# A hybrid decoder block on one core: the segments' openings traced in smaller pieces, B's serial products placed behind A's, and less scratch

## The chip, the core and the metric

The kernel runs on one core of a Trainium2 chip. The metric is the device time of one execution in microseconds (us). Engines are named as in the profile: PE is the matmul engine and PEld its weight loads, DVE the vector engine, ACT the scalar (activation) engine, POOL the GpSimd engine, and SP the engine that here only issues DMAs. Matmuls read from SBUF and write to PSUM, which has eight banks of 512 float32 columns by 128 partitions.

## The reference

One decoder block over 16 meta tokens and 1024 tokens, width 1024, all in float32:

```
h = h + 0.5 * swiglu(rmsnorm(h))                    # FFN 1, hidden width 2816
u = rmsnorm(h)
aq, ak, av, az, beta, alpha, bcols, ga, gb = split(u @ w_in)
o_a = deltanet(aq, ak, av, az, beta, alpha)         # "A": short causal convolution, silu, l2 norm,
                                                    #   chunked gated delta rule, 8 heads of 128
o_b = rwkv7(bcols)                                  # "B": token shift, low-rank decay, a and gate,
                                                    #   state recurrence, 16 heads of 64, group norm
h = h + (sigmoid(ga) * o_a + sigmoid(gb) * o_b) @ w_out
h = h + 0.5 * swiglu(rmsnorm(h))                    # FFN 2
return rmsnorm(h)[meta tokens dropped]
```

A chunk of A: with a triangular inverse T of the chunk, `v_new = u - w @ state`, `o = qg @ state + attn @ v_new`, `state = state * exp(g) + k_tail^T @ v_new`. B's state is carried over chunks of 64 tokens by one product with a chunk matrix.

## The kernel before

Activations lie with channels on partitions and tokens on the free axis. A float32 product is made as three products of rounded halves (high x high, high x low, low x high; `mm3`, recorded at line L262), so one projection of 128 output columns is 24 matmuls of up to 512 tokens; the tile of a projection is called `pp`, its weights `w` (loaded raw by SP as `wraw`, split by ACT L159 and DVE L160), its input tiles `uk`.

The program has three parts: FFN 1 (to about 736 us in the trace), the mixer (`middle`, to about 2300 us) and the output projection with FFN 2. The change touches only the mixer. It goes through two segments of tokens: segment 0 has the 16 meta tokens and 512 tokens (528 columns, done as 272 and 256), segment 1 the other 512. In each segment there are 8 steps, one for each pair of heads of B and one head of A, so 16 steps, numbered through (step 8 is the first of segment 1).

Each step is cut into acts, each a function that traces instructions:

- `new_b`: the low-rank decay (raw weights `upr` loaded, split to `upz`; products `pw` and `pa`; exponentials and a scan `Ls` on ACT and DVE), then B's three projections with the token shift (`vB`, `kB`, `rB`; function `shifted`), a transposition of vB (`vbp`), two column sums of the key (`cs`), and two of the bonus (`bon`).
- `new_a`: A's projections, convolution, silu and l2 norm.
- `operands`: the chunks' small products of both branches (`vap`, `grb`, `gra`, `bkt`, `vp`, `ktp`).
- `inverses`, `merge_blocks`, `transitions`: the triangular inverses, first row by row on DVE (`tb`, `Xb`), then in blocks of 32 and 64 on PE (`iv1` to `iv4`), then the products that make B's chunk matrices (`xp`, `vp`, `mp`, `np`).
- `chains`: the serial part. A has four chunks of 128, each with products p1, p2, pq (twice) and p3: p1, then a subtraction on DVE (`rhA`), p2, a scaling on ACT (`vn`), pq and p3, then the state's update on DVE (`SA`). B has eight chunks of 64, each one product b1 and one DVE operation (`SBs`); `bq` reads all of them.
- `gates` (three projections and `gat`) and `finish` (norms, merge, store).
- `segment(1)` loads and scales the new segment's input, makes `uk`, and calls `lora`, which makes the low-rank inputs shared by the 8 steps (`ws`, `as`, the gate's `gds` and `g3`, and by a scan `c3`, A's log decays) and transposes c3 to tokens on partitions (`tkp`).

The order in which acts are traced is given by the strings FIRST, REGULAR, BEFORE_SWITCH, SWITCH (a plus sign means the next step's). The tile framework's scheduler, at build time, then orders each engine's instructions by the traced order and its own model of durations; on the chip each engine runs its list in that order, and waits on semaphores. Tiles are allocated from pools: a tile's next use waits until its last reader is done. Scratch tiles of 528 columns come from one tag `tmp` with 8 slots. The projections' PSUM tiles come from `main_banks` (L239): two tiles of two banks in segment 0, three tiles of one bank in segment 1; two more banks serve the chains.

## Time and profile before

| what | us |
|---|---|
| median of 3 runs (range) | 3064.41 (3064.28 to 3066.05) |
| the profiled execution, its own time | 3063.9 |
| its span in the trace | 3062.1 |
| PE busy | 2946.3 |
| DVE busy | 2017.1 |
| ACT busy | 1377.8 |
| one step of segment 1, from `iv1` to `iv1` (1924.1 to 2011.1) | 87 |

A row of the order of time gives start, length, engine, line, operation, output and inputs by the program's names, the number of records, and in brackets how long the engine had been idle and what ended that. The rows count most matmuls twice, since a float32 product with plain operands is two passes. A row of a stretch gives its length, the busy time of PE, PEld, DVE, ACT and POOL with the number of records, the clock that was granted to PE (1.00 is full speed), the DMA share and GB/s. The granted clock is 0.99 over the whole execution.

### The profile page before, as it was taken

The numbers are of one execution on the slowest core, as the hardware profiler recorded it, in microseconds if no ns is written. First come the engines' busy times: TensorE is split into PE (matmuls) and PEld (weight loads), VectorE is DVE, ScalarE is ACT, GpSimd is POOL, SyncE is SP. The second block draws the span as 40 slices with busy tenths as digits, with TensorE's granted clock in tenths as the row PEclk, the third lists the DMA queues.
The fourth block names the chain that finished last, engine by engine and source line by source line (L and its number), as shares of the span: only waits on it lengthen the run. The fifth ranks groups of instructions, "written<-read, shape, count | busy, mean of one in ns | idle before, by whom it ended". The sixth has DMA issues, their size and how long they took to land. (4 is left out here: it accounts for less than half of the span.)

```text
span 3062.1 us, 61716 instructions
## 1 busy us (share of the span) xinstructions
PE 2946.3 (96%) x25498; PEld 2531.0 (83%) x25498; DVE 2017.1 (66%) x3872; ACT 1377.8 (45%) x2404; POOL 336.1 (11%) x503
## 2 busy tenths in 40 slices
PE   8999999999899999999999999999999999999998
PEld 8999998998778887888776777777777888888886
DVE  7555554346668877788768888877866765556335
ACT  5322222125555656566566556665644432223114
POOL 0322220000000000000000000000000022222000
PEclk9999999999999999999999999999999999999999
DMA  3232224234232322323323332233354232225223
GB/s 124 84 98 84 84 81 160 80 98 143 69 75 72 83 62 73 79 79 87 89 85 81 78 81 70 79 82 85 104 152 167 71 108 90 83 83 197 61 78 115
DMA packets 257594, 287.20 MB, mean 94 GB/s; under 512 B 169296, under 2 KB 175440, under 8 KB 257312
## 3 DMA queue, kind: packets, MB, share of 16 engines
q1 hardware_dynamic: 253072, 271.43, 30.2%
q0 software_dynamic: 2512, 8.65, 0.8%
q8 instruction: 201, 3.29, 0.5%
q10 hardware_dynamic: 1728, 3.16, 0.3%
q14 instruction: 81, 0.66, 0.1%
HBM read 232.70 MB, written 50.47 MB: 92 GB/s over the span
## 5 line engine op out<-in xcount | busy, mean ns | idle before, releaser
L262 PE MATMUL pp<-uk,w 128*128 128x512 f32 (+2 forms) x4824 | 969.0, 347 | 11.4 <-DVE w L160 7.4
L262 PEld LDWEIGHTS pp<-uk,w 128*128 128x128 f32 x4824 | 748.6, 191 | 105.9 <-DVE w L160 9.4
L159 ACT ACTIVATE w<-wraw 128x1024 fp32r<-128x1024 f32 (+2 forms) x330 | 326.5, 990 | 522.8 <-PE pd L262 296.8
L262 PE MATMUL pd<-hd,w 128*128 128x512 f32 (+2 forms) x2448 | 455.4, 347 | 5.5 <-ACT hd L159 3.7
L160 DVE TENSOR_TENSOR w<-wraw,w 128x1024 fp32r<-128x1024 f32 (+2 forms) x330 | 404.3, 1226 | 67.9 <-ACT w L159 57.2
L262 PEld LDWEIGHTS pd<-hd,w 128*128 128x128 f32 x2448 | 392.7, 190 | 64.0 <-ACT hd L159 3.9
L449 PE MATMUL pg<-bt,w 128*128 128x256 f32 (+2 forms) x2520 | 400.7, 317 | 0.0
L449 PEld LDWEIGHTS pg<-bt,w 128*128 128x128 f32 x2520 | 360.4, 188 | 33.0 <-DVE w L160 0.2
L455 DVE TENSOR_TENSOR c<-c,pg 128x520 f32<-128x520 f32 (+1 forms) x280 | 189.7, 689 | 278.0 <-PE pg L449 250.5
L449 PE MATMUL pg<-b,w 128*128 128x256 f32 (+2 forms) x2160 | 347.8, 317 | 0.0
L449 PEld LDWEIGHTS pg<-b,w 128*128 128x128 f32 x2160 | 309.7, 188 | 28.1
L159 ACT ACTIVATE w<-wrx 128x1024 fp32r<-128x1024 f32 (+1 forms) x64 | 58.5, 913 | 289.8 <-PE pg L449 249.2
L419 POOL TENSOR_TENSOR wrx<-wrx 128x512 f32<-128x512 f32 x38 | 52.5, 1382 | 733.1 <-DVE w22b L160 516.4
L1384 DVE TENSOR_TENSOR tb<-Ub,Xb 115x126 f32<-115x126 f32 (+22 forms) x496 | 124.9, 252 | 9.8 <-DMA Ub<-scr 1.4
L1386 DVE TENSOR_TENSOR Xb<-Xb,tb 115x126 f32<-115x126 f32 (+22 forms) x496 | 125.3, 253 | 8.2
L1193 DVE SCALAR_TENSOR_TENSOR acc<-xr,pk,acc 128x528 f32<-128x528 f32 (+1 forms) x144 | 109.4, 759 | 29.0 <-ACT acc L1189 27.8
L625 DVE SCALAR_TENSOR_TENSOR h<-pd,h 128x528 f32<-128x528 f32 (+1 forms) x64 | 44.6, 698 | 118.0 <-PE pd L262 115.4
L625 DVE SCALAR_TENSOR_TENSOR hh<-pd,hh 128x512 f32<-128x512 f32 x64 | 44.1, 690 | 115.5 <-PE pd L262 114.1
L262 PE MATMUL pwo<-uk,w 128*128 128x512 f32 x384 | 99.1, 408 | 3.4 <-DVE w L160 1.9
L262 PEld LDWEIGHTS pwo<-uk,w 128*128 128x128 f32 x384 | 72.1, 193 | 20.6 <-DVE w L160 2.3
L943 ACT ACTIVATE sh<-pp,pk 128x528 f32<-128x528 f32 (+1 forms) x54 | 37.5, 695 | 99.2 <-PE pp L262 99.1
L160 DVE TENSOR_TENSOR w<-wrx,w 128x1024 fp32r<-128x1024 f32 (+1 forms) x64 | 66.6, 1041 | 14.5 <-ACT w L159 14.3
(400 smaller groups left out, 4184.0 us busy)
## 6 DMA issues: line engine op xcount, KB each, us to landing
wraw<-in_win SPq DMA_DIRECT2D x150, 512.0 KB
wraw<-in_wgu SPq DMA_DIRECT2D x44, 512.0 KB
wrx<-in_wgu SPq DMA_DIRECT2D x44, 512.0 KB
wraw<-in_wdn SPq DMA_DIRECT2D x48, 320.0 KB
wraw<-in_wdn SPq DMA_DIRECT2D x32, 384.0 KB
hid<-c SPq DMA_DIRECT2D x44, 260.0 KB
hr<-hid SPq DMA_DIRECT2D x22, 520.0 KB
hid<-c SPq DMA_DIRECT2D x44, 256.0 KB
```

What stands on the lines that cost most here:

```text
L159: g.nc.scalar.activation(hi, src, AF.Copy)
L160: (eng or g.nc.vector).tensor_tensor(lo, src, hi.bitcast(F32), op=ALU.subtract)
L262: g.nc.tensor.matmul(ps, lhsT=l, rhs=r, start=i == 0, stop=i == n - 1)
L419: sums.tensor_tensor(a22, a21, a22, op=ALU.add)
L449: nc.tensor.matmul(ps[:, c0 : c0 + cn], lhsT=l[:, x, k, :], rhs=r[:, k, y, c0 : c0 + cn], start=i == 0, stop=i == 3 * HK - 1)
L455: nc.vector.tensor_tensor(o, x, y, op=ALU.add)
L625: nc.vector.scalar_tensor_tensor(hv, pd, 0.5, hv, op0=ALU.mult, op1=ALU.add)
L943: nc.scalar.activation(sh[:, 1 : 1 + n], ps, AF.Identity, scale=g.V("mu", i))
L1193: nc.vector.scalar_tensor_tensor(acc[:, :n], xr[:, tap : tap + n], V("convw", ct * 4 + tap), acc[:, :n], op0=ALU.mult, op1=ALU.add)
L1384: nc.vector.tensor_tensor(tv, U[:, i, i + 1 :].unsqueeze(2).to_broadcast([npt, nt, ncc]), X[:, i, 0:ncc].unsqueeze(1).to_broadcast([npt, n ...
L1386: nc.vector.tensor_tensor(X[:, i + 1 :, 0:ncc], X[:, i + 1 :, 0:ncc], tv, op=ALU.add)
```

## The change

Three edits, none of which adds or removes an instruction on any engine.

1. *Openings.* `new_b` is cut in two: `decay` (raw weights, `pw`, `pa`, exponentials, scan and what follows from it) and `new_b` (the rest). From `lora` the transposition of c3 is cut out as `tokens`. The acts are traced in a new order: at the first opening the decay of step 1 comes ahead of the operands of step 0, and `tokens` behind B's projections; at the second opening the PSUM banks are switched ahead of the last gates of segment 0, not behind them, and `tokens` again comes behind `new_b`.
2. *Chain.* B's products b1 are traced to come right behind A's p1 and p2 of each chunk, two to a chunk.
3. *Scratch.* `shifted` writes its result into the shift tile itself, the gate of the convolution goes into the convolution's input tile, and the raw low-rank weights get their own tile of 256 columns with one buffer, shared by the decay and the gates.

```diff
+FIRST = "decay new_b tokens new_a decay+ operands inverses new_b+ new_a+"
-FIRST = "new_b new_a operands inverses", "new_b new_a"
-REGULAR = "merge_blocks transitions operands+ inverses+ chains gates finish new_b++ new_a++"
-BEFORE_SWITCH = "merge_blocks transitions operands+ inverses+ chains gates finish gates+ segment new_b++ new_a++"
+REGULAR = "merge_blocks transitions operands+ inverses+ chains gates finish decay++ new_b++ new_a++"
+BEFORE_SWITCH = "merge_blocks transitions operands+ inverses+ chains gates finish banks gates+ segment decay++ new_b++ tokens++ new_a++"
...
+            elif act == "banks":
+                main_banks(g, 1, S1)
+            elif act == "decay":
+                steps[it] = decay(g, it)
...
-    main_banks(g, *((1, S1) if s else (2, 2)))
+    if s == 0:
+        main_banks(g, 2, 2)
...
-    o = g.st.tile([P, 531], F32, name=name, tag=tag, bufs=NTMP if tag == "tmp" else 1)
-    sh = tmp_tile(g, "sh", 529)
+    sh = tmp_tile(g, name if tag == "tmp" else "sh", 529)
+    o = sh if tag == "tmp" else g.st.tile([P, 531], F32, name=name, tag=tag)
...
-    raw = tmp("upr", 512).rearrange("p (a m) -> p a m", m=P)
-    nc.sync.dma_start(raw[:, 0:2, :], g.a["upwa"][j])
+    raw = st.tile([P, 2, P], F32, name="upr", tag="upr")
+    nc.sync.dma_start(raw, g.a["upwa"][j])
...
-        sg = tmp("sg")
+        sg = xr
...
+        m = nc.tensor.matmul(p1[:, :P], lhsT=kqg[:, 0, csl], rhs=S, start=True, stop=True)
         rh = st.tile([P, P], F32, name="rhA", tag="rhA", bufs=1)
         nc.vector.tensor_tensor(rh, Va[:, i, :], p1[:, :P], op=ALU.subtract)
+        with g.tc.issue_after(m.ins):
+            chunk_b(2 * i)
         p2 = pt("p2")
+        m = nc.tensor.matmul(p2[:, :P], lhsT=Y[:, NCB + i, :], rhs=rh, start=True, stop=True)
+        with g.tc.issue_after(m.ins):
+            chunk_b(2 * i + 1)
...
-    for i in range(NCB):
+    def chunk_b(i):
         ps = pt("b1")
         nc.tensor.matmul(ps[:, :CB], lhsT=g.mt[:, i], rhs=SBs[:, i], start=True, stop=True)
...
-        if i % 2 == 0:
-            chunk_a(i // 2)
+    for i in range(NCA):
+        chunk_a(i)
...
-    raw = tmp_tile(g, "ugr", 512).rearrange("p (a m) -> p a m", m=P)
+    raw = st.tile([P, 2, P], F32, name="ugr", tag="upr")
```

What this makes of the engines' lists. A row is line, operation, output and inputs, shape, and how many in a row; `pp` is a projection. The first place is PE's list at the opening of segment 0, from A's value product of step 0 (`vap`) on. Before:

```order
L1205 MATMUL vap<-ck,acc 128x128 x4
L1210 MATMUL vmp<-ck,acc 16x128
L262 MATMUL pp<-uk,w 128x256 x2
L1231 MATMUL grb<-AR,BK 64x128 x32
L1241 MATMUL gbm<-arm,bkpm 64x16 x2
L1270 MATMUL gra<-kq 128x256 x4
```

and further down, behind the products `bkt`, `vp`, `btp`, `ktp` and `vmp` with no `pp` among them:

```order
L1332 MATMUL vmp<-ck,kq 16x128
L1103 MATMUL pw<-ws,upz 128x256
L1104 MATMUL pw<-ws,upz 128x256
L1107 MATMUL pa<-as,upz 128x256
L1108 MATMUL pa<-as,upz 128x256
L1103 MATMUL pw<-ws,upz 128x272
L1104 MATMUL pw<-ws,upz 128x272
L1107 MATMUL pa<-as,upz 128x272
L1108 MATMUL pa<-as,upz 128x272
L1076 MATMUL vbp<-ck,vB 64x64 x16
```

Now, from the second half of the decay's products on (the first half stands right behind `vap`, too):

```order
L1115 MATMUL pa<-as,upz 128x272
L1116 MATMUL pa<-as,upz 128x272
L261 MATMUL pp<-uk,w 128x256 x2
L1247 MATMUL grb<-AR,BK 64x128 x16
L261 MATMUL pp<-uk,w 128x256 x5
L1247 MATMUL grb<-AR,BK 64x128 x16
L1257 MATMUL gbm<-arm,bkpm 64x16 x2
L1286 MATMUL gra<-kq 128x256 x4
L261 MATMUL pp<-uk,w 128x272 x9
L1296 MATMUL gm<-c3m,ck 16x16
L261 MATMUL pp<-uk,w 128x272 x8
```

The decay's products of step 1 have moved ahead of all of step 0's operands, and 51 projection products stand between `vap` and `vbp`, where there were two.

The second place is PE's list at the opening of segment 1, from the last gates of segment 0 (`gat` closes them) to the decay of step 8. Before:

```order
L262 MATMUL pp<-uk,w 128x512 x24
L1601 MATMUL gat<-gds,ug 128x512 x3
L1601 MATMUL gat<-g_7380,ug 128x512
L262 MATMUL pp<-uk,w 128x512 x103
L999 MATMUL tkp<-ck,c_17710 128x16 x4
L1103 MATMUL pw<-ws,upz 128x512
```

Now:

```order
L261 MATMUL pp<-uk,w 128x512 x29
L1623 MATMUL gat<-gds,ug 128x512 x2
L261 MATMUL pp<-uk,w 128x512 x22
L1623 MATMUL gat<-gds,ug 128x512
L1623 MATMUL gat<-g_7377,ug 128x512
L261 MATMUL pp<-uk,w 128x512 x72
L1111 MATMUL pw<-ws,upz 128x512
```

`tkp` no longer stands ahead of `pw` (it is now behind the first `bon` of step 8), and `gat` stands among the last gate projection. A few projections have changed sides of `gat`; their sum is the same.

The third place is PE's list in a chunk of the chain in a regular step of segment 1. Before:

```order
L1562 MATMUL b_22825<-SBs,mt 128x64
L1542 MATMUL p_22828<-SA,kq 128x128
L262 MATMUL pp<-uk,w 128x512 x3
L1546 MATMUL p_22832<-rhA,Y_7140 128x128
L1550 MATMUL pq<-kq,SA 128x128
L262 MATMUL pp<-uk,w 128x512 x2
L1551 MATMUL pq<-attn,vn 128x128
L1553 MATMUL p_22839<-vn,ktl 128x128
L262 MATMUL pp<-uk,w 128x512
L1562 MATMUL b_22843<-SBs,mt 128x64
```

Now (p1, b1, p2, b1, pq, pq, p3):

```order
L1558 MATMUL p_22720<-SA,kq 128x128
L1583 MATMUL b_22724<-SBs,mt 128x64
L261 MATMUL pp<-uk,w 128x512 x2
L1564 MATMUL p_22727<-rhA,Y_7140 128x128
L1583 MATMUL b_22729<-SBs,mt 128x64
L261 MATMUL pp<-uk,w 128x512 x2
L1570 MATMUL pq<-kq,SA 128x128
L1571 MATMUL pq<-attn,vn 128x128
L1573 MATMUL p_22737<-vn,ktl 128x128
L261 MATMUL pp<-uk,w 128x512 x3
```

B's two products have moved from between p3 and the next p1 into the two links behind p1 and p2, and the cover of each link changed from 3, 2 and 4 or 5 `pp` to 2, 2 and 3. Around step 9, where segment 1's second step begins, 33 `pp` stand between step 8's `bq` and step 9's first `bon`, where there were 59.

More of the change, by code (lines that the diff above doesn't have):

```diff
@@ L170, in schedule @@
     yield "segment", 0
-    for it in range(2):
-        for act in FIRST[it].split():
-            yield act, it
+    for act in FIRST.split():
+        yield act.rstrip("+"), act.count("+")
     for it in range(last + 1):
@@ L1078, in run, with decay @@
     return out
-def new_b(g, it):
+def decay(g, it):
     nc, st, V = g.nc, g.st, g.V
@@ L1125, in new_b @@
         nc.scalar.activation(elm[:, 1:17], Ls[:, 0:16], AF.Exp, scale=-CDEC)
+    q.EN, q.ELx, q.av = EN, ELx, av
+    return q
+def new_b(g, q):
+    nc, st, V, c, j, n, off, it = g.nc, g.st, g.V, q.c, q.j, q.n, q.off, q.it
+    meta = q.s == 0
+    fs = slice(off, off + FULL)
+    tmp = lambda name, w=528: tmp_tile(g, name, w)
+    EN, ELx, av, elm = q.EN, q.ELx, q.av, meta and q.elm
     v = shifted(g, c, 48 + j, 16 + j, "vB")
@@ L1168, in new_b @@
     nc.vector.tensor_tensor(bv, ps, v[:, fs], op=ALU.mult)
-    return q
 def new_a(g, q):
```

16 lines of the change are left out of this document (8 added, 8 removed).

## The prediction

> **What bounds the kernel now.** I read the page's sums first, then the chain that ended last, then the span cut into stretches, and last the order of time on the matmul engine (PE) where a stretch showed idle time.
>
> ```profile
> span 3062.1 us, 61716 instructions
> PE 2946.3 (96%) x25498; PEld 2531.0 (83%) x25498; DVE 2017.1 (66%) x3872; ACT 1377.8 (45%) x2404; POOL 336.1 (11%) x503
> ...
> PE 37%; DVE 3%; ACT 2%; issue 1%; DMA 1%; SPq 0%; DVEq 0%; ACTq 0%
> ```
>
> PE is busy 96% of the span, and the chain is mostly PE. No instruction is added or removed by this change, so it can only win back time in which PE stands still or runs at a lower clock. Where that time lies, by stretches (columns: length, then busy time of PE, weight loads, DVE, ACT, POOL; then the granted clock):
>
> ```profile
> 700.00:900.00 200.00, 178.97 (x1705) 160.67 (x1707) 136.40 (x269) 117.55 (x212) 12.31 (x53) 0.97 0.32 95
> 900.00:1500.00 600.00, 579.42 (x7072) 497.44 (x7063) 465.08 (x1156) 348.43 (x715) 35.82 (x133) 1.00 0.29 77
> 1500.00:1700.00 200.00, 179.95 (x1881) 141.79 (x1880) 146.14 (x322) 122.22 (x220) 17.27 (x37) 0.94 0.30 79
> 1700.00:2300.00 600.00, 579.12 (x6358) 460.22 (x6358) 475.72 (x1132) 348.26 (x669) 34.86 (x90) 1.00 0.35 92
> ...
> 832.07:842.30 10.23, 8.32 (x62) 7.48 (x63) 9.26 (x33) 3.32 (x8) 0.48 (x5) 0.50 0.00 1
> 862.79:866.19 3.40, 3.40 (x17) 3.40 (x16) 3.40 (x12) 1.68 (x4) 0.23 (x2) 0.50 0.78 252
> 1511.32:1514.72 3.40, 3.40 (x9) 2.63 (x9) 3.40 (x10) 2.29 (x4) 0.00 (x0) 0.50 0.42 162
> 1545.46:1552.26 6.80, 4.79 (x15) 4.18 (x16) 2.73 (x6) 2.66 (x5) 0.48 (x2) 0.50 0.04 14
> 1654.68:1664.90 10.22, 6.93 (x16) 5.07 (x16) 10.04 (x24) 5.51 (x10) 0.66 (x1) 0.50 0.28 103
> 1685.40:1688.80 3.40, 3.40 (x67) 3.26 (x68) 2.41 (x8) 0.66 (x2) 0.30 (x1) 0.50 0.17 24
> ```
>
> The two segment openings (700 to 900, 1500 to 1700) have 21.0 and 20.1 us of idle PE in 200 us each; the 1200 us of regular steps between and behind them have 41.5 us, about 3 us in each of some 13 steps. The last six rows are the only stretches of the mixer at half clock, and all lie in the openings. PE's busy time in them is 30.2 us, of which half, 15.1 us, is lost. So the openings hold 41 + 15 = 56 us, and those are the places that the traced order is changed in.
>
> **The first opening.** PE's rows in order of time (start, length, engine, operation, and in brackets the idle time ahead with what ended it):
>
> ```profile
> 736.93 22.85 PE L262 MATMUL pp<-uk,w 128*128 128x272 f32 x183
> 761.25 1.04 PE L999 MATMUL tkp<-ck,c 128*128 128x16 f32 x8 [1.47 <-ACT g L993]
> ...
> 810.19 0.50 PE L262 MATMUL pp<-uk,w 128*128 128x256 f32 x2
> 813.55 1.69 PE L1231 MATMUL grb<-AR,BK 64*64 64x128 f32 x32 [1.70 <-DVE LT L1234]
> 833.25 1.13 PE L1076 MATMUL vbp<-ck,vB 64*64 64x64 f32 x32 [4.70 <-DVE vB L944]
> 836.09 0.61 PE L1138 MATMUL vbm<-ck,vB 128*16 128x128 f32 x2 [0.73 <-ACT Vs L1135]
> 861.60 5.73 PE L262 MATMUL pp<-uk,w 128*128 128x272 f32 x32 [2.93 <-DVE w L160]
> ...
> 809.00:836.80 27.80, 16.36 (x272) 12.15 (x272) 15.67 (x45) 13.98 (x34) 0.95 (x8) 0.91 0.21 54
> 809.00:861.60 52.60, 37.88 (x420) 32.94 (x420) 37.35 (x106) 23.84 (x49) 2.77 (x13) 0.90 0.14 39
> ```
>
> From 809.0 to 836.8 PE idles 27.80 - 16.36 = 11.4 us: the operands of step 0 go round over DVE and ACT with two projection products (pp) as the only cover, and then the decay of step 1 does the same, ending in 4.70 us before `vbp`. In the new order the decay products of step 1 stand right behind `vap`, so their exponentials and the scan run beside the operands, and the 4.70 and 0.73 us lose their cause. Among the operands now stand 51 pp of 256 or 272 columns. By the row of 183 in 22.85 us each is 0.125 us, so they fill 51 x 0.125 = 6.4 us of the other 11.4 - 5.4 = 6.0 us. They will not fit exactly, because they come in blocks of 2 to 9 and the decay's ACT work now queues among the operands' own: I leave 3 us idle, a gain of 8.4. With the 4.70 us gone the half clock from 832.07 (8.32 busy, 4.2 lost) goes too, but I leave one 3.4-us stretch of it (1.7). **Term 1: 8.4 + 4.2 - 1.7 = -11 us.** DVE bounds it: it has 37.35 us of work in the 52.60 us up to the wait for a weight split at 861.60, so no more than 15 us can go. That wait I leave as it is, since what comes earlier on PE meets the same splits on DVE. If DVE and ACT swallow most, 4 us remain: bounds -4 to -15.
>
> The token products of the opening (`tkp`, 761.25) move behind the column sums `bon`, where c has long been there: **term 2: -1.5 us** (0 to -1.5).
>
> [...] Half clock after a wait is shown by 832.07 (4.70 us), 1511.32 and 1545.46 (3.35 and 3.94, below), but also by 1685.40, behind a wait of 1.70 us. [...]
>
> **The second opening.**
>
> ```profile
> 1511.11 7.35 PE L262 MATMUL pp<-uk,w 128*128 128x512 f32 x24 [3.35 <-ACT gs L952]
> 1524.85 15.48 PE L262 MATMUL pp<-uk,w 128*128 128x512 f32 x67 [0.41 <-DVE uk L160]
> 1547.47 1.86 PE L999 MATMUL tkp<-ck,c 128*128 128x16 f32 x8 [3.94 <-DVE c L985]
> 1549.17 0.77 PE L1103 MATMUL pw<-ws,upz 128*128 128x512 f32 x1
> ```
>
> The 3.35 us are the second gate projection of step 7 waiting for one of two double-bank tiles to be read. With the switch to three single-bank tiles ahead of the gates there is a third tile, so this wait goes, and the half clock at 1511.32 (3.40 busy, 1.7 lost) with it: 5.0. What is late next is the new segment's input: its tiles `uk` are written as the last gate product lets go of the old ones, and 0.41 us of wait for them stand at 1524.85 already. I keep half a microsecond for it. **Term 3: -4.5 us** (-1 to -5).
>
> At 1547.47 PE waits 3.94 us for the scan that makes c, then the decay products follow. In the new order `tkp` stands behind `bon` of step 8, so PE goes from the last input projection straight to `pw`, whose weights `upz` are now made before the gates' projections end. The 1.86 us of `tkp` are work that only moves. Gone are 3.94 us and the half clock at 1545.46 (4.79 busy, 2.4 lost): 6.3, less a little for DVE. **Term 4: -6 us** (-3 to -6.3). If `upz` came only where it comes now, `pw` would wait about half of this: the lower bound.
>
> **Step 9, where the order speaks against the change.**
>
> ```profile
> 1635.70 1.15 PE L1570 MATMUL bq<-AR,SBs 64*64 64x64 f32 x32
> 1644.90 0.40 PE L1023 MATMUL cs<-hl,bdr 128*128 128x512 f32 x1
> 1645.13 5.21 PE L262 MATMUL pp<-uk,w 128*128 128x512 f32 x22
> 1654.27 0.49 PE L1023 MATMUL bon<-hl,bdr 128*128 128x512 f32 x1 [1.59 <-ACT hl L159]
> 1658.85 7.20 PE L262 MATMUL pp<-uk,w 128*128 128x512 f32 x18 [2.86 <-DVE w L160]
> 1640.00:1663.00 23.00, 17.88 (x65) 13.05 (x65) 23.00 (x55) 12.41 (x19) 2.88 (x3) 0.82 0.21 73
> ```
>
> DVE is busy for all of these 23 us: the inversion's rows (tb, Xb), the end of step 8 and the operands of step 9 share it. From `bq` to `bon` it takes 1654.27 - 1635.70 = 18.6 us. Before, PE has 59 pp there (by 22 in 5.21 us, 0.237 us each: 14.0 us, and about 2.5 us of other products) and so waits about 2 us. Now it has 33 pp (7.8 us), and DVE has as much to do: PE would wait 18.6 - 7.8 - 2.5 = 8.3 us, 6.3 more than now. Against it, `w` of the next projection now comes ahead of `bon` on DVE (2.86 us less), and 17 of the 26 pp missing here now stand between the stages of the next inversion (between `iv1` and `vap`, for 1 before), where PE had almost no cover, and where the half clock of 1685.40 (1.7 lost) is, behind a wait of 1.70 us. The half clock at 1654.68 (3.5 lost) stays in some form. 6.3 - 2.9 - 1.9, the last for part of these 3.4: **term 5: +1.5 us**, with -4 if DVE runs ahead because the opening ends sooner, and +8 if nothing comes back.
>
> **The regular steps: B's products in A's chain.** A chunk of the chain before:
>
> ```profile
> 1961.75 0.44 PE L1542 MATMUL p<-SA,kq 128*128 128x128 f32 x2
> 1961.94 0.94 PE L262 MATMUL pp<-uk,w 128*128 128x512 f32 x3
> 1962.72 0.38 PE L1546 MATMUL p<-rhA,Y 128*128 128x128 f32 x2
> 1963.63 0.42 PE L1551 MATMUL pq<-attn,vn 128*128 128x128 f32 x2
> 1963.88 0.39 PE L1553 MATMUL p<-vn,ktl 128*128 128x128 f32 x2
> 1965.60 0.44 PE L1542 MATMUL p<-SA,kq 128*128 128x128 f32 x2
> 1964.31 0.35 DVE L1554 SCALAR_TENSOR_TENSOR SA<-SA,egl,p 128x128 f32<-128x128 f32 x1 [1.79 <-PE p L1553]
> 1924.10:2011.10 87.00, 83.54 (x947) 66.47 (x948) 70.61 (x166) 52.72 (x102) 5.96 (x15) 1.00 0.31 82
> ```
>
> No wait over 0.2 us is shown. From p1 to p2 there are 0.97 us with 3 pp; now b1 (0.17) and 2 pp (0.47) behind p1's own 0.19: 0.83, so 0.14 us short. From p3 to the next p1 there are 1.72 us, with two b1 and 4 pp; now 3 to 5 pp, 0.85 to 1.3 us, and the update of the state on DVE ends 0.78 us after p3's start, so this link is barely held. If every such link is short by 0.14 to 0.2 us, four chunks cost 1.4 us a step, 22 us in 16 steps. On the other side the whole chain has fewer pp in it (34 for 38), and `iv1` now has 34 in front of it behind the first `bon`, for 16, so the 3.5 us that a step idles can shrink: by 0.7 us in 14 steps, 10 us. I take the middle of what happens in most links, nothing: **term 6: 0 us** (-10 to +22).
>
> The scratch edits (values in place, gate in the convolution's tile, own tile for the raw weights) add no instruction; they free slots, which lets the orders above be found, and get no term of their own. The shared raw-weight tile has one buffer for the decay's and the gates' raw weights, but in the new order its load stands half a step ahead of `pw`, so SP hides it.
>
> **Sum:** -11 - 1.5 - 4.5 - 6 + 1.5 + 0 = -21.5, from the profiled execution's 3063.9 us (span 3062.1): 3042.4. The three runs have a median of 3064.4, 0.5 above it: **3043 us**.
>
> **Rivals.** *The chain loses its cover (slower).* b1 stands between p1 and p2, and between p2 and pq, and every chunk has one link that waits on DVE's order: a chain update that stands behind one row of the inversion or one 128x512 operation there. At 0.5 us a chunk it is 2 us a step, 32 us in 16 steps: 3043 + 32 = 3075. It decides from 21.5 / 16 = 1.35 us a step on. For it: DVE is busy 70.61 of 87.00 us. Against it: no link waits now, and the chunk's length in pp (9) stays the same. Chance 0.12.
>
> *DVE is the next bound in both openings (no change).* Terms 1 and 3 at their small ends (-4, -1), term 4 at -3, step 9 at +8: 0 us, 3064. For it: DVE full at 1640 to 1663 and the two waits for weight splits. Against it: DVE has 15 us to spare in the first opening. Chance 0.12.
>
> *The regular steps gain too.* Term 6 at -10 and term 1 at -15: 3043 - 14 = 3029. It counts as part of the forecast's side; chance 0.16. The forecast itself, 3034 to 3058, has 0.60.
>
> **How the numbers follow.** Under 0.2% (6 us) a difference can't be told from none here. Faster: 0.60 + 0.16 = 0.76; same 0.12; slower 0.12. The range leaves out the slower rival and a tail below the sum's low side: 3024 to 3064.
>
> **What would show it.** Right: no wait of 3 us or more ahead of `vbp`, the gate projection and `pw`; half clock in the openings well under 37 us; a wait of some 8 us ahead of `bon` of step 9; regular steps of seg 1 at 87 us. Wrong: waits of 0.3 us or more ahead of p2 or p1 in most chunks and steps of 88.5 us or longer, or a wait for `uk` or `w` as long as the one taken away.

## The result, and the profile after

The changed kernel takes **3049.4 us** (median of 4 executions, 3048.2 to 3052.7), the kernel before 3065.2 us beside it (4 executions, 3064.3 to 3068.3). The ratio is 0.9950 with a 95% interval of 0.9938 to 0.9963, so the change is faster by 0.5%, 16 us where 21 were forecast. The profiled execution took 3048.16 us.

The sums of its page, and its chain of waits:

```profile
span 3046.4 us, 61663 instructions
PE 2942.3 (97%) x25498; PEld 2530.1 (83%) x25498; DVE 2007.7 (66%) x3872; ACT 1372.2 (45%) x2404; POOL 348.6 (11%) x503
...
PE 52%; DVE 10%; ACT 5%; issue 2%; DMA 1%; SPq 0%; DVEq 0%; ACTq 0%
```

No work has gone from PE: it is busy 4.0 us less, in a span 15.7 us shorter. To see where, I cut both spans at the same pieces of work: at the first projection of the mixer, at the first `bq` of steps 1, 6, 7, 8 and 15, and at the output projection. The kernel before, from the mixer's start to step 8, in stretches (columns as in the prediction's stretches; the long one from step 1 to step 6 is left out):

```profile
733.14:1021.47 288.33, 264.01 (x2973) 232.50 (x2971) 201.48 (x472) 169.05 (x331) 15.98 (x72) 0.98 0.28 75
...
1501.00:1635.70 134.70, 123.52 (x1127) 97.04 (x1126) 95.74 (x207) 84.69 (x150) 11.18 (x23) 0.96 0.28 76
1635.70:1720.56 84.86, 75.92 (x861) 60.30 (x860) 69.01 (x178) 49.63 (x95) 6.28 (x15) 0.92 0.28 72
```

and the changed kernel:

```profile
731.75:1013.09 281.34, 261.54 (x2946) 228.92 (x2944) 196.46 (x468) 164.09 (x323) 18.99 (x74) 0.98 0.28 75
...
1485.87:1612.98 127.11, 123.98 (x1139) 98.91 (x1138) 95.63 (x210) 82.63 (x151) 9.80 (x24) 0.99 0.31 83
1612.98:1689.67 76.69, 66.42 (x830) 51.86 (x829) 59.95 (x148) 41.44 (x80) 4.31 (x10) 0.96 0.29 70
```

The lengths alone mislead, since projections have moved across the cuts: in the new kernel the stretch to `bq` of step 7 has 12 more PE records than before, the one behind it 31 fewer. So I count the **lost time** of a stretch: its length, less the PE work that lies in it, each instruction at the median distance to the next that its kind has in the trace of before. It holds idle time, half clock and crowding (products that follow one another more slowly than usual) alike. How finely kinds are told apart moves the level of a stretch by up to 13 us and the difference between two programs by up to 1.6 us, so the differences are what to read. "Again" is a second profile of the same changed kernel (from one of the runs below), which shows what two executions of one program differ by. In us:

| stretch | forecast of the change | lost before | lost after | again |
|---|---|---|---|---|
| FFN 1, up to the first projection | 0 | 21.6 | 20.2 | 19.3 |
| first opening, to `bq` of step 1 | -12.5 (terms 1, 2) | 61.2 | 57.6 | 59.8 |
| steps to `bq` of step 6 | 0 (term 6) | 76.2 | 73.4 | 73.3 |
| second opening, to `bq` of step 7 | -10.5 (terms 3, 4) | 27.4 | 17.1 | 17.3 |
| to `bq` of step 8, with step 9's `bon` | +1.5 (term 5) | 22.7 | 21.7 | 22.2 |
| segment 1, to `bq` of step 15 | 0 (term 6) | 87.6 | 87.4 | 86.6 |
| last step, output projection, FFN 2 | 0 | 11.1 | 14.8 | 14.1 |
| sum | -21.5 | 307.8 | 292.1 | 292.7 |

Two profiles of one program agree within about 2 us a stretch. So the second opening gave what was forecast, the first three tenths of it or less, and the end lost 3 us that nobody had on the list. FFN 1, which the change doesn't touch, differs by 1.4 us.

PE's rows of the changed kernel in order of time, where it waits or where the prediction had a wait (in brackets the idle time ahead, and what ended it):

```profile
846.25 5.50 PE L261 MATMUL pp<-uk,w 128*128 128x272 f32 x30 [1.91 <-DVE w L160]
864.08 2.07 PE L261 MATMUL pp<-uk,w 128*128 128x512 f32 x4 [3.26 <-DVE w L160]
951.06 1.87 PE L261 MATMUL pp<-uk,w 128*128 128x272 f32 x13 [2.23 <-ACT acc L1205]
1483.20 0.49 PE L1564 MATMUL p<-rhA,Y 128*128 128x128 f32 x2 [1.04 <-DVE rhA L1560]
1553.81 0.96 PE L1008 MATMUL tkp<-ck,c 128*128 128x16 f32 x8
1631.86 0.79 PE L1032 MATMUL bon<-hl,bdr 128*128 128x512 f32 x1 [7.60 <-ACT hl L159]
2301.70 1.73 PE L1032 MATMUL cs<-hl,bdr 128*128 128x512 f32 x2 [2.82 <-ACT hl L1046]
```

The 4.70 us ahead of `vbp`, the 3.35 ahead of the gate projection and the 3.94 ahead of `tkp` are gone; at `bon` of step 9 stand 7.60 us. New are the wait for a weight split at 846 and the one for `acc` at 951; the wait for a split at 864 has 3.26 us where the kernel before had 2.93 at 861.60. Three short stretches of the changed kernel, and as the last row the second one in the kernel before:

```profile
809.00:836.80 27.80, 26.32 (x360) 22.81 (x359) 18.77 (x47) 16.70 (x37) 1.79 (x8) 1.00 0.23 56
832.00:868.00 36.00, 30.52 (x187) 26.92 (x186) 34.38 (x90) 24.38 (x42) 4.44 (x7) 0.91 0.21 67
...
1863.41:1950.60 87.19, 84.00 (x942) 66.84 (x941) 70.42 (x167) 52.86 (x102) 8.01 (x15) 1.00 0.31 82
...
832.00:868.00 36.00, 30.74 (x225) 29.16 (x226) 32.28 (x93) 17.08 (x29) 3.78 (x11) 0.81 0.15 45
```

Up to 836.8 the forecast holds: PE is busy 26.3 us at full clock, for 16.4 at 0.91 before, a gain of 26.3 - 16.4 x 0.91 = 11.4 us against 11 in term 1. But from 832 to 868 DVE, which was thought to have time to spare, is busy 34.38 of 36 us, PE waits for it twice, and the clock is 0.91. The third row is a regular step of segment 1: 87 us as before. The last row says that DVE had little room there to begin with: 32.28 of the same 36 us.

What got worse there is the order on DVE. The row-by-row inversion of step 0 (`tb` and `Xb`, 31 rows that wait for one another, some 15 us of work in both kernels) takes DVE from 831.88 to 866.83 in the kernel before and from 828.78 to 872.46 now: 43.7 us (44.6 in the second profile) for 35.0. Between its rows stand 46 other operations with 30.7 us by their records, where there were 29 with 20.3. So the first product that needs it comes later, before and now, although PE has run ahead:

```profile
878.56 0.74 PE L1419 MATMUL iv<-Xc,LT 32*32 32x32 f32 x32 [0.34 <-DMA Xc<-scX]
...
885.39 0.75 PE L1435 MATMUL iv<-Xc,LT 32*32 32x32 f32 x32 [1.92 <-DMA Xc<-scX]
```

The first `bq` of step 0 then starts at 931.69, for 931.67 before.

### The profile page after: what moved, and what is told of

Read it like the earlier page. It is cut to its first block, busy times and chain, and to the rows that moved or that the text cites. A ratio compares the mean times of both kernels' runs of the same rounds, so it can differ in the third digit from the quotient of the medians.

```text
span 3046.4 us, 61663 instructions
## 1 busy us (share of the span) xinstructions
PE 2942.3 (97%) x25498; PEld 2530.1 (83%) x25498; DVE 2007.7 (66%) x3872; ACT 1372.2 (45%) x2404; POOL 348.6 (11%) x503
## 4 chain that ended last, share of the span: by engine, by line
PE 52%; DVE 10%; ACT 5%; issue 2%; DMA 1%; SPq 0%; DVEq 0%; ACTq 0%
PE pp L261 16%; PE pg L448 13%; PE pd L261 8%; PE pwo L261 3%; PE pg L472 1%; DVE w L160 1%; DVE tb L1400 1%; DVE Xb L1402 1%; ACT w L159 1%; PE vp L1085 1%; PE cs L1032 1%; PE mp L1085 1%; PE np L1085 1%; DVE mt L1508 1%; PE bkt L1317 1%
## 5 line engine op out<-in xcount | busy, mean ns | idle before, releaser
L261 PEld LDWEIGHTS pp<-uk,w 128*128 128x128 f32 x4824 | 741.3, 190 | 105.5 <-DVE w L160 13.2
L624 DVE SCALAR_TENSOR_TENSOR h<-pd,h 128x528 f32<-128x528 f32 (+1 forms) x64 | 44.6, 698 | 116.4 <-PE pd L261 116.4
L160 DVE TENSOR_TENSOR w<-wrx,w 128x1024 fp32r<-128x1024 f32 (+1 forms) x64 | 66.6, 1041 | 14.9 <-ACT w L159 14.8
L159 ACT ACTIVATE hd<-hr 128x1040 fp32r<-128x1040 f32 (+1 forms) x40 | 41.2, 1061 | 63.3 <-DMA hr<-hid 38.3
```

The costliest lines, as they stand in the source:

```text
L159: g.nc.scalar.activation(hi, src, AF.Copy)
L160: (eng or g.nc.vector).tensor_tensor(lo, src, hi.bitcast(F32), op=ALU.subtract)
L261: g.nc.tensor.matmul(ps, lhsT=l, rhs=r, start=i == 0, stop=i == n - 1)
L624: nc.vector.scalar_tensor_tensor(hv, pd, 0.5, hv, op0=ALU.mult, op1=ALU.add)
```

## The experiments

Three questions. Which of the three edits gives the gain, and do their shares add? What took the gain of the first opening back: DVE, which is full there, or the order and clock of PE? And what became of the small terms (PSUM banks, step 9, the last step)? Each ratio is against the kernel before, run beside it, with its 95% interval; diffs are against the changed kernel. "Lost" is the count of the table above.

**The openings' order alone.** The chain and the scratch tiles are as before.

```diff
-    sh = tmp_tile(g, name if tag == "tmp" else "sh", 529)
-    o = sh if tag == "tmp" else g.st.tile([P, 531], F32, name=name, tag=tag)
+    o = g.st.tile([P, 531], F32, name=name, tag=tag, bufs=NTMP if tag == "tmp" else 1)
+    sh = tmp_tile(g, "sh", 529)
...
-        sg = xr
+        sg = tmp("sg")
...
+    for i in range(NCB):
+        if i % 2 == 0:
+            chunk_a(i // 2)
```

> The kernel before with the new order of acts alone (decay, tokens, banks), the chain and the scratch as before. Theory A (each part's gain is its own): the second opening wins its 10 us (no wait of 3 us ahead of the gate projection and of pw), the first opening 4 us, the regular steps and the end of the mixer stay: 13 to 14 us faster than the kernel before. Theory B (the scratch slots are what lets the openings fill): less than half of that, 0 to 6 us faster.

Measured: 3067.7 us, ratio 1.0005 (0.9996 to 1.0013): no gain at all. Yet its openings do gain: lost time to `bq` of step 1 is 56.3 (before 61.2), in the second opening 20.7 (27.4), to step 8 20.8 (22.7), 13.5 us together. The steps lose it again: 80.8 in segment 0 (76.2) and 99.2 in segment 1 (87.6), 16.2 us. They are not lost in all steps, but next to the second opening: in segment 0 in the last two steps, in segment 1 some 3 us in the first step and 8 in the second. The second step and the third, then PE and ACT in the second:

```profile
1791.70:1891.18 99.48, 92.88 (x959) 73.00 (x959) 73.54 (x171) 56.53 (x109) 6.47 (x15) 0.97 0.28 73
1891.18:1977.67 86.49, 83.14 (x940) 66.22 (x939) 70.84 (x168) 52.38 (x102) 5.67 (x15) 1.00 0.32 82
...
1804.22 0.73 PE L261 MATMUL pp<-uk,w 128*128 128x512 f32 x2 [2.17 <-ACT w L159]
...
1802.61 0.61 ACT L1127 ACTIVATE ELx<-Ls 128x512 f32<-128x512 f32 x1
1803.13 1.04 ACT L159 ACTIVATE w<-wraw 128x1024 fp32r<-128x1024 f32 x1
```

The weight split on ACT (1803.13) stands behind ten activations, eight of them the decay's, from 1797.4 to 1803.1, with no idle time ahead of it, and PE waits 2.17 us. The third step is as long as in the kernel before (86.82 us). So without the scratch edits the scheduler's list next to the second opening is a worse one; that it is for want of slots is argued, not shown.

**The chain's order alone.** Openings and scratch as before.

```diff
-FIRST = "decay new_b tokens new_a decay+ operands inverses new_b+ new_a+"
+FIRST = "new_b new_a operands inverses", "new_b new_a"
...
-    if s == 0:
-        main_banks(g, 2, 2)
+    main_banks(g, *((1, S1) if s else (2, 2)))
...
-    sh = tmp_tile(g, name if tag == "tmp" else "sh", 529)
+    o = g.st.tile([P, 531], F32, name=name, tag=tag, bufs=NTMP if tag == "tmp" else 1)
```

> The kernel before with B's products behind A's p1 and p2 alone. Theory A: about 1 us a step less in the steps of segment 0 (6 to 7 us in all), nothing in segment 1's regular steps, and the end of the mixer (the last chain and the output projection) 3 to 4 us longer: 2 to 4 us faster in all. Theory B (the chain's links lose cover): each regular step 1 us or more longer, 10 us slower or worse. Theory C (the longer end has nothing to do with the chain): no change at the end.

Measured: 3060.0 us, 0.9978 (0.9969 to 0.9987). The second opening's lost time is 22.8 (27.4) although the wait for the gates' tile is still there (4.00 us at 1518.63); the steps of segment 0 lose 77.6 (76.2), segment 1 87.0 (87.6), the end 13.9 (11.1). So the gain isn't where theory A had it, in the steps of segment 0.

**The scratch edits alone.** Openings and chain as before; nothing else differs.

```diff
-FIRST = "decay new_b tokens new_a decay+ operands inverses new_b+ new_a+"
+FIRST = "new_b new_a operands inverses", "new_b new_a"
...
+    for i in range(NCB):
+        if i % 2 == 0:
+            chunk_a(i // 2)
```

> The kernel before with the scratch edits alone. Theory A: no gain of its own, within 3 us of the kernel before. Theory B (slots are what held PE up): 5 us faster or more, with 1 us a step less in segment 0, and the first opening better covered (its order has 31 projection products among step 0's operands, for 2).

Measured: 3063.2 us, 0.9990 (0.9981 to 0.9999): at most a small gain. The first opening loses more (65.8 for 61.2), the second far less (18.9 for 27.4), though PE still waits there for the gates' tile and for `tkp`:

```profile
1519.08 21.11 PE L262 MATMUL pp<-uk,w 128*128 128x512 f32 x85 [3.53 <-DVE gg L1602]
1545.71 1.04 PE L999 MATMUL tkp<-ck,c 128*128 128x16 f32 x8 [1.43 <-DVE c L985]
```

**Openings and scratch, without the chain's order.**

```diff
-        with g.tc.issue_after(m.ins):
-            chunk_b(2 * i)
...
-    for i in range(NCA):
-        chunk_a(i)
+    for i in range(NCB):
+        if i % 2 == 0:
+            chunk_a(i // 2)
```

> The changed kernel with the chain as it was before. Its order has 37 projection products ahead of step 9's bon, for 3. Theory A: no wait of 7 us ahead of step 9's bon (5 us less), the end of the mixer 3 to 4 us shorter, the steps of segment 0 about 1 us longer each (6 to 7 us more): within 4 us of the changed kernel, 3045 to 3052. Theory B (the chain edit carries the gain): 3055 or more. Theory C (step 9's stall comes from DVE being full, not from the order): the wait ahead of bon stays at 4 us or more.

Measured: 3053.2 us, 0.9958 (0.9944 to 0.9972). That is 4 us over the changed kernel, though its six executions spread from 3048.9 to 3059.7. The steps of segment 0 lose 77.5 (73.4 with the chain's order), segment 1 88.8 (87.4), while the second opening is at 15.5 (17.1) and the end at 12.5 (14.8). At step 9 there are 37 `pp` ahead of `bon` and its wait is split up:

```profile
1637.05 0.50 PE L1032 MATMUL bon<-hl,bdr 128*128 128x512 f32 x1 [0.75 <-ACT hl L159]
1638.35 0.50 PE L1032 MATMUL bon<-hl,bdr 128*128 128x512 f32 x1 [0.80 <-DVE hl L160]
1641.84 4.21 PE L261 MATMUL pp<-uk,w 128*128 128x512 f32 x9 [2.52 <-DVE w L160]
```

The stretch loses 22.8 us, with the single 7.60-us wait 21.7: the same total in other pieces.

**Chain and scratch, without the openings' order.**

```diff
-FIRST = "decay new_b tokens new_a decay+ operands inverses new_b+ new_a+"
-REGULAR = "merge_blocks transitions operands+ inverses+ chains gates finish decay++ new_b++ new_a++"
+FIRST = "new_b new_a operands inverses", "new_b new_a"
+REGULAR = "merge_blocks transitions operands+ inverses+ chains gates finish new_b++ new_a++"
```

> The order of the products and all of the scratch edits, without the new order of the openings' acts. Theory additive: the two parts alone gave -5.8 and -2.7 us, so together about -8.5, 3056 to 3058 us, and the openings' order then adds some 7 us to make the changed kernel. Theory shared: the two parts remove the same waits at the second opening (each left one of 3.5 to 4.0 us there), so the second one is worth nothing more and the time is 3059 to 3062 us. Theory enough: the two carry the whole gain and the order of the openings adds nothing, 3050 us or less.

Measured: 3059.8 us, 0.9982 (0.9973 to 0.9991), inside the middle expectation: beside the chain the scratch edits are worth nothing. The gates' wait is back (3.91 us at 1516.81), and the first opening loses 65.6.

In one table, medians in us (the kernel before had 3065 to 3066 beside each of them):

| | openings as before | openings in the new order |
|---|---|---|
| neither | 3065.8 | 3067.7 |
| chain | 3060.0 | not run |
| scratch | 3063.2 | 3053.2 |
| chain and scratch | 3059.8 | 3048.8 (nine executions) |

The shares do not add. The openings' order costs 2 us or nothing alone, and gains 10 and 11 us where the scratch edits are in.

**Four weight splits computed twice.** Each of the first opening's four splits on DVE is issued a second time, with the same inputs and output: 4 x 1.22 = 4.9 us more DVE work.

```diff
+TWICE = [("win", ct, 1) for ct in (1, 17, 24, 59)]
...
+    if at in TWICE:
+        g.nc.vector.tensor_tensor(w[:, 1, :kk, :], raw[:, :kk, :], w[:, 0, :kk, :].bitcast(F32), op=ALU.subtract)
```

> The changed kernel with each of the four weight splits of the first opening on the VectorE computed twice, with the same result: 4 x 1.22 = 4.9 us of VectorE work more, all of it in about 800 to 870 us, nothing more on the TensorE. If the VectorE bounds the first opening, most of it comes out behind: 3 to 5 us over the changed kernel, 3052 to 3055 us, with longer waits for the weight halves and the gated operand between 845 and 880. If the TensorE's own order and the half clock bound it, the time is within 2 us of the changed kernel, 3048 to 3051 us.

Measured: 3054.5 us, 0.9959 (0.9947 to 0.9972), against 3048.8, 0.9944 (0.9932 to 0.9957) for the changed kernel on the same chip: 5.8 us between the medians for 4.9 us of work on an engine that is 66% busy over the span. The intervals touch, but five executions of 3052.5 to 3055.1 stand against five of which four are 3046.5 to 3049.8. Lost time to `bq` of step 1 is 62.7, for 57.6 and 59.8. The inversion of step 0 lasts 47.7 us on DVE, for 43.7 in the changed kernel, and all behind it is late:

```profile
889.78 0.75 PE L1439 MATMUL iv<-Xc,LT 32*32 32x32 f32 x32 [0.85 <-DMA Xc<-scX]
```

That is 4.4 us behind the changed kernel's 885.39, and `bq` of step 0 comes at 936.57, for 931.69. The order that the scheduler finds for PE differs a little too, so a part of it could be that; the size is that of the added work.

**Splits on POOL.** Six splits, the four of the first opening and two at step 9, go from DVE to POOL.

```diff
+ON_POOL = [("win", ct, 1) for ct in (1, 17, 24, 59)] + [("win", ct, 2) for ct in (1, 17)]
...
-    split(g, raw[:, :kk, :], w[:, 0, :kk, :], w[:, 1, :kk, :])
+    split(g, raw[:, :kk, :], w[:, 0, :kk, :], w[:, 1, :kk, :], eng=g.nc.gpsimd if at in ON_POOL else None)
```

> The changed kernel, with the low halves of six weight splits (the projections around 845 to 866 us, and two of step 9) computed on POOL, which is idle there, and not on DVE. Theory D (after the change DVE's full queue is what PE waits for in both places): the waits of 1.9 and 3.3 us ahead of these projections and their half clock shrink to under 2 us together, and the wait ahead of step 9's bon falls from 7.6 us to 5 or less: 4 to 9 us faster than the changed kernel, 3040 to 3046. Theory P (what stands in PE's list is the bound): within 3 us of it. Theory O (POOL's longer operation, or its share of DVE's access, costs what it saves): slower than it.

Measured: 3054.3 us, 0.9961 (0.9948 to 0.9973): no gain, rather 5 us more, as theory O had it. Two of POOL's rows, each with DVE's rows beside and behind it, and PE's:

```profile
842.33 2.71 POOL L160 TENSOR_TENSOR w<-wraw,w 128x1024 fp32r<-128x1024 f32 x1 [0.56 <-ACT w L159]
842.74 2.86 DVE L1211 SCALAR_TENSOR_TENSOR acc<-xr,pk,acc 128x528 f32<-128x528 f32 x1
846.50 0.75 DVE L1211 SCALAR_TENSOR_TENSOR acc<-xr,pk,acc 128x528 f32<-128x528 f32 x1
...
864.55 3.35 POOL L160 TENSOR_TENSOR w<-wraw,w 128x1024 fp32r<-128x1024 f32 x1 [3.30 <-ACT w L159]
865.56 2.49 DVE L1272 SCALAR_TENSOR_TENSOR E<-gp,tk,ck 128x128 f32<-128x128 f32 x1
868.16 0.34 DVE L1272 SCALAR_TENSOR_TENSOR E<-gp,tk,ck 128x128 f32<-128x128 f32 x1
...
843.35 0.79 PE L1034 MATMUL bon<-hl,bdr 128*128 128x512 f32 x1 [2.53 <-ACT hl L159]
859.62 0.52 PE L1034 MATMUL cs<-hl,onesr 128*128 128x256 f32 x2 [2.38 <-ACT hl L1048]
```

The long waits for `w` are gone, and 2.53 and 2.38 us for `hl` stand in their place. DVE was not freed: beside each of the four splits of the first opening one operation of DVE that began while POOL worked lasted until POOL was done, a `tb` 2.33 us for 0.24, an `acc` 2.86 us for 0.75, a `tb` 2.50 us for 0.29, an `E` 2.49 us for 0.34. In the first opening DVE's operations became 8.6 us longer in this way, for 4 x 1.22 = 4.9 us of splits taken off it. So the run doesn't tell whether PE's wait is that of the splits as such. It fits DVE as the bound, since more of DVE's time was taken than given back. At step 9 the wait of 7.60 us became 2.10 and others (1.15, 1.87, 0.94, 0.72), with 9.2 us of idle time in the stretch for 10.3.

**The decay of step 1 late.** Only the first opening changes: the decay stands behind the inverses, as before.

```diff
-FIRST = "decay new_b tokens new_a decay+ operands inverses new_b+ new_a+"
+FIRST = "decay new_b tokens new_a operands inverses decay+ new_b+ new_a+"
```

> The changed kernel with the decay of step 1 traced behind step 0's operands, as before. Its list has the decay's products right ahead of vbp again. Theory D (DVE bounds the first opening): the wait of 4.7 us ahead of vbp and the half clock of 10 us are back, but the later waits for weight splits shrink, so it is only 1 to 4 us slower than the changed kernel: 3050 to 3054. Theory of the prediction (what PE idles there is worth its full length): 9 to 12 us slower, 3058 to 3062.

Measured: **3044.2 us**, 0.9929 (0.9916 to 0.9941): faster than the changed kernel, which no expectation had. The wait that term 1 was about is back, and a half-clock stretch of 10 us with it (granted clock 0.50 from 827.9 to 838.1):

```profile
831.27 1.13 PE L1085 MATMUL vbp<-ck,vB 64*64 64x64 f32 x32 [4.78 <-DVE vB L946]
...
922.42:1013.69 91.27, 88.37 (x1105) 76.37 (x1104) 70.70 (x175) 54.36 (x110) 5.87 (x21) 1.00 0.29 76
```

The inversion of step 0 takes DVE 37.9 us, from 826.37 to 864.22, and its first product on PE and step 0's `bq` come 9 to 10 us earlier than in the changed kernel, at 875.73 and 922.42 for 885.39 and 931.69. Up to that `bq` both lose the same, 40.6 us here and 39.9 and 42.4 in the changed kernel's two profiles, so PE has done less other work by then. But then, to `bq` of step 1, PE idles 91.27 - 88.37 = 2.9 us at full clock. The changed kernel in the same stretch:

```profile
931.69:1013.09 81.40, 75.92 (x966) 63.02 (x965) 61.32 (x152) 45.93 (x94) 6.35 (x19) 0.98 0.27 66
```

5.5 us idle at 0.98: the row at 951.06 above, 2.23 us for the convolution's `acc`, is in it, and the late decay's trace has only 0.79 us there, for `w`. The late decay also loses 13.0 us in the second opening, for 17.1, where the traced order is the same and the list that the scheduler made of it is not, and 1.8 more in the stretch of step 9.

**The PSUM switch behind the gates, as before.**

```diff
-... chains gates finish banks gates+ segment decay++ new_b++ tokens++ new_a++"
+... chains gates finish gates+ segment decay++ new_b++ tokens++ new_a++"
...
-    if s == 0:
-        main_banks(g, 2, 2)
+    main_banks(g, *((1, S1) if s else (2, 2)))
```

> The changed kernel with the switch of the PSUM banks behind the last gates of segment 0, as before. Theory A (banks): a wait of 3.5 to 4 us ahead of a projection at the second opening is back, with a half clock of 3.4 us, as in the kernels with the chain or the scratch edit alone: 4 to 6 us slower than the changed kernel, 3053 to 3056. Rival (DVE is the bound there, too): within 2 us of the changed kernel.

Measured: 3052.5 us, 0.9954 (0.9941 to 0.9966), 3 us over the changed kernel, but the intervals overlap. It lies between the two theories. The wait is back:

```profile
1510.05 18.23 PE L261 MATMUL pp<-uk,w 128*128 128x512 f32 x72 [3.12 <-DVE gg L1623]
```

It costs 1.6 us of lost time in its own stretch (18.7 for 17.1), though idle time alone rises by 3.7.

**The old chain in the last step only.**

```diff
+    last = q.it == 2 * NJ - 1
...
-        with g.tc.issue_after(m.ins):
-            chunk_b(2 * i)
+        if not last:
+            with g.tc.issue_after(m.ins):
+                chunk_b(2 * i)
...
+        if last:
+            chunk_b(2 * i)
```

> The changed kernel with the chain of the last step (it = 15) as before: b1 between p3 and the next p1. All other lists are the same up to there. Theory A (the chain edit makes the end longer, because the last chain gets less of the output projection as cover and its norms come late): 2 to 3 us faster than the changed kernel, 3046 to 3047. Rival (the longer end comes from weights or DVE): within 1 us of it.

Measured: 3048.7 us, 0.9942 (0.9929 to 0.9956): the same as the changed kernel. The end loses 13.2, for 14.8 and 14.1.

**Both of these: late decay, old chain in the last step; and the changed kernel once more beside it.**

```diff
-FIRST = "decay new_b tokens new_a decay+ operands inverses new_b+ new_a+"
+FIRST = "decay new_b tokens new_a operands inverses decay+ new_b+ new_a+"
...
+        if last:
+            chunk_b(2 * i)
```

> The changed kernel with two edits together: the decays of a first step stand behind the inverses again (as in the run with the decay late, 3044.2 us), and the last recurrence step alone takes the old order of the two batches' products (3048.7 us against 3049.4 without that edit, with the last stretch 2.0 us shorter). If the two act in different places, as the traces say (first opening and last step), they add: 3041 to 3043 us. If the gain of the late decay came from the last step's phase and not from the opening, the old last order takes the same gain once more and the time stays at 3044 to 3045 us.

The changed kernel itself, with no edit:

> The changed kernel once more, word for word the same program, for a comparison with the other three on one chip: 3048 to 3052 us if what is told of differences of 3 to 5 us between runs of different calls stands; if it comes out at 3044 to 3046 us, the gain of the late decay was a difference between chips.

Measured on one chip: 3046.1 us, 0.9936 (0.9924 to 0.9949), and 3048.8 us, 0.9944 (0.9932 to 0.9957). So the two edits do not add: the end loses 14.0 us here, no less than with the new chain (13.0 with the late decay alone). The `cs` product of the last step waits less, and that is all that the old order buys:

```profile
2301.20 0.50 PE L1032 MATMUL cs<-hl,bdr 128*128 128x512 f32 x1 [2.18 <-ACT hl L1046]
```

2.18 us for 2.82. The late decay itself holds up as a small gain: its ten executions in both forms have a median of 3045.8 us, eight of them below 3047.4; the changed kernel's nine have 3048.8, one of them below 3047.4. In both of its profiles the stretch from `bq` of step 0 to `bq` of step 1 loses 13.9 us (17.7 and 17.5 in the changed kernel), and the second opening 13.0 and 13.9 (17.1 and 17.3). The fastest version is the changed kernel with the late decay alone, some 3 to 5 us under the change and about 20 under the kernel before.

## Why the prediction was right, and where it was not

**The sign and the bound were right.** PE had nothing to win but waits and half clock, and the openings were the place. All four signs named for it are there: no wait ahead of `vbp`, the gate projection or `pw`; 7.60 us ahead of step 9's `bon`; 87.19 us a step in segment 1; and 20.5 us of half clock in the openings (27.3 in the second profile), for 37.5. That the total is off by 6 us only is in part luck. By the table 12.8 us of the forecast were missed, nearly all in the first opening and at the end, and 6.9 came that were not forecast: 2.8 in segment 0, 2.5 at step 9, 1.4 in FFN 1 and 0.2 in segment 1.

**Terms 1 and 2 (-12.5) failed: -3.6, and -1.4 in the second profile.** The step that failed is "That wait I leave as it is, since what comes earlier on PE meets the same splits on DVE", with its bound from 37.35 us of DVE work in 52.60. The gain itself came, 11.4 us by 836.8. But a sum over 52 us does not say when the engine is free. DVE's spare time lay ahead of 836.8 (15.67 us busy of 27.80 before); from 832 to 868 it was nearly full before (32.28 of 36 us) and is fuller now. There the earlier work stands between the rows of step 0's inversion, which lasts 43.7 us for 35.0, so that step 0's `bq` is no earlier than before although PE was 11 us ahead. The waits for `w` grow from 2.93 us to 1.91 + 3.26, each with 3.4 us of half clock behind it (granted clock 0.50 from 847.0 to 850.5 and from 864.1 to 867.5); then come 1.92 us for the inversion's result, for 0.34, and in step 1 2.23 us for `acc`. ACT's half of the split and DVE's, ahead of the second wait:

```profile
857.24 1.08 ACT L159 ACTIVATE w<-wraw 128x1024 fp32r<-128x1024 f32 x1
...
861.84 0.34 DVE L1270 SCALAR_TENSOR_TENSOR E<-gp,tk,ck 128x128 f32<-128x128 f32 x1
862.55 0.26 DVE L1402 TENSOR_TENSOR Xb<-Xb,tb 115x110 f32<-115x110 f32 x1
862.80 1.22 DVE L160 TENSOR_TENSOR w<-wraw,w 128x1024 fp32r<-128x1024 f32 x1
```

ACT is done at 858.3 and DVE comes to its half at 862.8, behind the convolution, the inversion's rows and the operands. That DVE's amount of work counts there is shown by the doubled splits (4.9 us in, 5.8 out). That the inversion is the link is supported by three runs in one order: it lasts 37.9 us with the late decay, 43.7 in the changed kernel and 47.7 with the splits doubled, and step 0's `bq` comes at 922.42, 931.69 and 936.57. No run changed the inversion alone, so this much is argued. Whether the splits themselves matter more than other work of DVE, the POOL run can't tell. That the early decay gives nothing in the end is shown by the run that traces it late again: 3 to 5 us faster. Why the late decay also helps at the second opening, 600 us later, is open.

**Terms 3 and 4 (-10.5) came out: -10.3 and -10.1.** The split between them is not confirmed. With the banks switched late the gates' wait is back and costs 1.6 us in its stretch (3 between the medians), where term 3 said 4.5. And the scratch edits alone win 8.5 us there with both waits still standing, at 3.53 and 1.43 us. So the sum is right and its parts are only argued, and its agreement can be luck: part of it is half clock and crowding that other lists shed as well.

**Term 5: the wait was right (7.60 us for 8.3), the sum too high** (-1.0 and -0.5 for +1.5). Three lists gave this stretch 7.60 us in one piece, 0.75 + 0.80 + 2.52 and more, or 2.10 and four others, and each loses 21.7 to 22.9 us, for 22.7 before. The equal sums suggest that the cover which was moved away from `bon` covers elsewhere, as the prediction's terms of -2.9 and -1.9 had it, and that these were too small; no run shows it place by place.

**Term 6 (0): right in segment 1** (87.4 and 86.6 for 87.6), a little low in segment 0 (-2.8). The rival in which the chain loses its cover falls: undoing the chain's order makes the steps of segment 0 lose 4.1 us more, and 1.4 in segment 1. The argument that a chunk's nine `pp` stay the same was loose, since the chain as a whole went from 38 to 34; no link came to wait for it.

**Not foreseen: the end, +3.7 and +3.0.** Eight profiles with the new chain throughout lose 13.0 to 15.2 us there, four with the old one throughout 11.0 to 12.5. Of that, 0.65 us is the longer wait of the last step's `cs` (2.82, for 2.17 in the kernel before), and 0.78 us a wait for `rg` at 2304.21, where the kernel before has none of 0.2 us or more. The last step's own order does not decide the rest, since with only that undone the end loses 13.2 and 14.0. The half clock that stands there twice lasts longer, too (3.4 us each time before, 6.8 in the changed kernel). The prediction's list of half clock left these two out, as lying behind the mixer, but the first stands at the last step's own `cs`. Before:

```profile
2320.00:2327.00 7.00, 6.49 (x21) 4.94 (x22) 5.46 (x8) 2.78 (x5) 0.00 (x0) 0.76 0.74 250
2354.00:2361.00 7.00, 7.00 (x25) 5.56 (x25) 1.99 (x3) 1.62 (x3) 0.00 (x0) 0.76 0.60 187
```

and in the changed kernel, at the same two products:

```profile
2301.00:2308.00 7.00, 5.38 (x11) 3.61 (x12) 5.13 (x8) 2.09 (x5) 0.00 (x0) 0.51 0.89 313
2335.00:2342.00 7.00, 5.96 (x14) 4.70 (x15) 3.32 (x4) 1.15 (x2) 0.00 (x0) 0.52 0.59 183
```

As busy time by what is missing of the clock, 6.49 x 0.24 + 7.00 x 0.24 = 3.2 us are lost before and 5.38 x 0.49 + 5.96 x 0.48 = 5.5 after, 2.3 of the 3.7. Why it lasts longer stays open; in the second profile the second of the two stretches is again as short as before (3.4 us, the first 6.8).

**The scratch edits had "no term of their own".** That they only free slots was right as to what they do, and they gain 3 us at most alone. But the prediction took it that the openings would gain by their order, and the runs show that this order gains nothing without them. Most of what the scratch edits buy lies in the steps next to the second opening, not in the openings: with that order the steps of the two segments lose 80.8 and 99.2 us without the scratch edits, 77.5 and 88.8 with them, and the second opening 20.7 and 15.5.

## What to carry to other kernels

Where a wait in front of a busy engine is removed, look at the feeding engine in the stretch that comes next, not at its average over the whole opening, and ask between which serial operations the earlier work will stand: the time won can be handed back a few tens of microseconds later. Undo each part of a change with the others in place, since parts that share slots and a scheduler do not add: here one of them was worth -2 us alone and +10 beside another, and one that did what it said was better left out.

## What the runs showed of the hardware

*The same wait, another length of half clock.* The following shows two profiles of the changed kernel, each around its wait for `w` at 864 (3.26 and 3.25 us), and around 885. The first:

```profile
862.00:870.00 8.00, 5.92 (x48) 4.03 (x49) 6.79 (x19) 4.20 (x9) 1.15 (x1) 0.79 0.41 131
885.00:892.00 7.00, 6.61 (x136) 6.14 (x137) 2.45 (x6) 3.00 (x7) 1.33 (x5) 1.00 0.28 43
```

and the second, whose trace runs 0.86 us earlier here:

```profile
861.20:869.20 8.00, 5.98 (x33) 4.00 (x37) 6.25 (x18) 4.16 (x9) 1.15 (x1) 0.59 0.42 131
885.00:892.00 7.00, 6.47 (x108) 5.89 (x110) 2.27 (x4) 2.51 (x6) 1.59 (x5) 0.76 0.36 53
```

With the same program and nearly the same waits the granted clock is 0.79 in the one and 0.59 in the other. A little later it is 1.00 and 0.76, there behind a wait for `Xc` of 1.92 us in the first profile and of only 1.65 us in the second. This goes some way to explain why a stretch is known to 2 us only. The clock is granted at 0.50 for 3.4 us in the first profile (864.1 to 867.5) and for 6.8 us in the second (862.6 to 869.4). By these lengths 3.4 us at half clock in 8 us make 0.79, and the 6.6 us of the second that lie in its stretch make 0.59. What decides between the two lengths was not shown. Nor does half clock come only behind waits of that size: behind the wait of 1.04 us at 1483.20 the clock falls,

```profile
1484.00:1488.00 4.00, 3.73 (x41) 3.07 (x41) 2.75 (x11) 1.52 (x4) 0.00 (x0) 0.67 0.41 145
```

with PE busy 2.75 of the 4 us ahead of it (1480 to 1484), in products most of which have 128 columns or fewer.

*A split on POOL* took 2.71 and 3.35 us in the rows above, on DVE 1.22 us (862.80 in the changed kernel), for the same 128 x 1024 elements. Beside it DVE was held up: an operation of 0.75 us took 2.86, one of 0.34 us 2.49, each until the split on POOL was done, and so it went beside the other two splits of the first opening (2.33 us for 0.24, 2.50 for 0.29).
